# Seven-product blocks in four gated FFNs and two mixers: two of four weight sums moved from VectorE to accumulating transfers, with another order of products and another first block

## The chip, the cores and the metric

The kernel runs on one core of a Trainium2 chip. The metric is the device time of one execution in microseconds (us). Its engines are TensorE (PE in the profile, with PEld for its weight loads), VectorE (DVE), ScalarE (ACT), GpSimd (POOL) and SyncE (SP). They run their own instruction queues and wait for one another by semaphores. SP, ACT and POOL can each issue transfers (DMA), which 16 DMA engines carry out.

## What is computed

Two transformer blocks over one sequence of 256 tokens of width 1024, all in float32. Each block is half a gated FFN, a mixer and half a gated FFN, with an RMS norm ahead of each; the second one ends in a norm.

```python
x = x + 0.5 * swiglu(rms_norm(x, ffn1_norm), w_gate, w_up, w_down)     # FFN 1
x = x + concat(attention_with_top_64(h), pooled(h)) @ w_out            # mixer 1, h = rms_norm(x) @ w_in
x = x + 0.5 * swiglu(rms_norm(x, ffn2_norm), ...)                      # FFN 2
x = x + 0.5 * swiglu_2(rmsnorm(x, ffn1_norm_2), ...)                   # FFN 3
x = x + hybrid_mixer(rmsnorm(x, mix_norm_2), ...)                      # mixer 2
x = x + 0.5 * swiglu_2(rmsnorm(x, ffn2_norm_2), ...)                   # FFN 4
x = rmsnorm(x, final_norm_2)

def swiglu(x, w_gate, w_up, w_down):                                   # 1024 -> 2816 -> 1024
    return (silu(x @ w_gate) * (x @ w_up)) @ w_down
```

## The kernel before

Tokens lie in two tiles t of 128, the width in 8 tiles k of 128. Float32 precision is had from float32r matmuls: every operand is split into a rounded part `hi` (ACT copies it, L80) and the rest `lo` (DVE subtracts, L81), and a product is three matmuls (`mm3`, L83). `weights` (L65) loads 128x2048 float32, 1 MB, by SP into one of two `raw` buffers, and `parts` splits it into one of three pairs of `whi` and `wlo`.

An FFN (`ffn`, L300) has gate and up columns in blocks j of 512 (the last, j = 5, of 256 gate and 256 up columns). A plain block takes gate (G) and up (U) in halves c of four k: one weight load, 24 matmuls of 512 columns for each half, four halves in all, two for block 5. `plain` (L321) is a generator that hands back after each half. Blocks 1 and 3 are done by `quad` (L156): G and U times two halves of the width, two by two blocks, with seven products of 12 matmuls in place of eight. It loads b11, b12, b22, b21 as w11, w12, w22, w21 into four `block` buffers, forms sums of them on DVE (L180, L183, L188, L197) and multiplies them with the sums and differences of x that `combined` (L136) left split in `xc`. Results are joined by DVE (L186 to L202). It hands back after each product. `ORDER` (L35) lists for two groups of blocks whose next step comes: 0 the seven-product block, 1 and 2 the plain ones.

Ahead of the groups the first block, j = 0, is done: G half 0, U half 0, G half 1, U half 1, with `combined` before the last. In FFN 1 `cold_start` (L279) does G half 0 in four pieces as they land. `gated` (L308) takes silu, scales by `rstd` and multiplies; `turned` (L205) transposes the product (eight 128x128 transposes with `ident`) and splits it into `act`. It is put off by `later` and done by a `flush` some steps on. Then the down product runs over `act` in six weight loads for each 512 columns, and `add` (L251) adds it to X.

`mixer1` (L403) projects by `products`, loads tables (`mixer1_tables`, L384) by POOL, forms q and k tables on DVE (L397, L400), and applies the rope (L382) to the index projections. `rsqrt` (L96) ends in a POOL operation. The last lines of `run` (L810 to L828) scale by the final norm and store in four pieces by SP.

The kernel is written for a framework that gives each engine its queue, sets all semaphores and may put an instruction ahead of others of the text where its operands are there earlier; buffers of one tag are given out as they come free.

Of the kernel before, what the change touches and what calls it, by code (L numbers as in the profile page):

```python
# [17 lines left out]
P = 128  # L18
T = 256
# [22 lines left out]
class Block:  # L42
# [81 lines left out]
    def rows(self, accs, w, x, k0, nk, last, n=512):  # L124

        for t in range(2):
# [29 lines left out]
    def quad(self, pool, b, x, xc):  # L156
# [32 lines left out]
        ps = product(of_xc(2), self.parts(w12))  # L189
        tt(y21, ps, y12, op=ALU.add)  # L190
        tt(y12, y12, y22, op=ALU.add)
        tt(y22, y21, y22, op=ALU.add)
        yield
        ps = product(of_xc(3), self.parts(w22))
        tt(y12, ps, y12, op=ALU.add)
# [4 lines left out]
        yield  # L200
        ps = product(of_x(1, 0), self.parts(w21))
        tt(y11, ps, y11, op=ALU.add)  # L202
        return [y11, y21], [y12, y22]
# [47 lines left out]
    def add(self, accs, f, scale, following):  # L251
# [3 lines left out]
        for t in range(2):  # L255
# [4 lines left out]
        for t in range(2):  # L260
            self.squares(t, f)
# [16 lines left out]

    def cold_start(self, accs, src):  # L279

        nc = self.nc
        raw = self.block()
        hi = self.wsp.tile([P, 2048], F32R, tag="whi", name="whi")
        lo = self.wsp.tile([P, 2048], F32R, tag="wlo", name="wlo")
        xT = self.block().rearrange("p (k t) -> p k t", t=T)
        self.hT = self.big.tile([P, KD, 2, T], F32R, tag="hT", name="hT")
        for k in range(4):
            s = slice(k * 512, k * 512 + 512)
            if k % 2 == 0:
                nc.sync.dma_start(xT[:, k : k + 2, :], self.a["xT"][:, k : k + 2, :])  # L290
            nc.sync.dma_start(raw[:, s], src[:, s])
            self.feed(k, xT[:, k, :], "ffn1_norm")
            self.split(hi[:, s], lo[:, s], raw[:, s])
            for t in range(2):
                self.mm3(accs[t], self.both(self.hT[:, k, :, t * P : t * P + P]), (hi[:, s], lo[:, s]), k == 0, False)
        nc.sync.dma_start(xT[:, 4:8, :], self.a["xT"][:, 4:8, :])
        for k in range(4, KD):
            self.feed(k, xT[:, k, :], "ffn1_norm")

    def ffn(self, n, following, first=False):  # L300
        nc, a = self.nc, self.a
        gu, d, d_end = a[f"gu{n}"], a[f"d{n}"], a[f"de{n}"]
        with self.stage(4), self.tc.tile_pool(name="act", bufs=1) as pool:
# [4 lines left out]
            def gated(j, gs, us):  # L308
# [8 lines left out]
                self.later(lambda: self.turned(act, prs, 4 * j), 2)  # L317
# [18 lines left out]
            def seven(j):  # L336
                gated(j, *(yield from self.quad(pool, [[gu[2 * j + i, c] for i in range(2)] for c in range(2)], self.hT, xc)))


            G = two()  # L340
            if first:
                self.cold_start(G, gu[0, 0])
            else:
                self.token_major(G, gu[0], 512, 0)
            self.flush()
            U = two()
            self.token_major(U, gu[1], 512, 0)
            self.flush()
            self.token_major(G, gu[0], 512, 1)
            if first:  # L350
                nc.sync.dma_start(self.ident, a["ident"])
                for t in range(2):
                    nc.sync.dma_start(self.X[t], a["x"][t])
                    for f in range(2):
                        self.squares(t, f)
            r = self.rstd()
            self.combined(xc, self.hT)
            self.token_major(U, gu[1], 512, 1)
            gated(0, G, U)

            for order, blocks in ORDER:
                steps = [seven(j) if kind == "s" else plain(j) for kind, j in blocks]
                for i in order:
                    next(steps[i], None)
                    self.flush(2 - (blocks[i][0] == "s"))
            for f in range(2):
                accs = [self.ps() for _ in range(2)]
                for c in range(6):
                    self.rows(accs, self.weights(d[f, c] if c < 5 else d_end[f]), act, 4 * c, 4 if c < 5 else 2, KF - 1)
                    self.flush(2)  # L370
                self.add(accs, f, 0.5, following)
# [12 lines left out]
    def mixer1_tables(self):  # L384
        nc, a, c1 = self.nc, self.a, self.c1
        load = lambda name, shape: self.load(c1, name, shape, nc.gpsimd)
        cosq, sinq = load("cosq", [P, 2, 64]), load("sinq", [P, 2, 64])
        self.cosi, self.sini = load("cosi", [P, 2, 32]), load("sini", [P, 2, 32])
# [536 lines left out]
```

## Time and profile before

| | us |
|---|---|
| device time, median of 3 runs | 1125.61 (1124.76 to 1126.65) |
| the profiled execution, device time | 1126.87 |
| its span, first to last instruction | 1125.1 |
| PE busy | 1079.1 (96%), 5154 matmuls |
| DVE busy | 790.3 (70%) |
| ACT busy | 568.1 (50%) |
| POOL busy | 22.0 (2%) |
| mean granted clock of TensorE | 0.985 |
| transfers | 201.76 MB, 179 GB/s over the span |

A busy PE counts overlapping matmuls once, so that a stretch with gaps shorter than a matmul counts as busy; the number of matmuls in a stretch tells more. Granted clock 1.00 is 2.4 GHz, 0.5 is 1.2 GHz.

### The profile page before, as it was taken

The numbers are of one execution on the slowest core, as the hardware profiler recorded it, in microseconds if no ns is written. First come the engines' busy times: TensorE is split into PE (matmuls) and PEld (weight loads), VectorE is DVE, ScalarE is ACT, GpSimd is POOL, SyncE is SP. The second block draws the span as 40 slices with busy tenths as digits, with TensorE's granted clock in tenths as the row PEclk, the third lists the DMA queues.
The fourth block names the chain that finished last, engine by engine and source line by source line (L and its number), as shares of the span: only waits on it lengthen the run. The fifth ranks groups of instructions, "written<-read, shape, count | busy, mean of one in ns | idle before, by whom it ended". The sixth has DMA issues, their size and how long they took to land.

```text
span 1125.1 us, 12742 instructions
## 1 busy us (share of the span) xinstructions
PE 1079.1 (96%) x5154; PEld 895.0 (80%) x5154; DVE 790.3 (70%) x785; ACT 568.1 (50%) x632; POOL 22.0 (2%) x42
## 2 busy tenths in 40 slices
PE   6899999899999999998999999999999998999996
PEld 4788888778876788886777888999888887778785
DVE  6889744597589986458997555677645467998543
ACT  6465534568355654434565444543444345566432
POOL 0000000220000000000000000000000000000000
PEclk8999999989999999999999999999999999999999
DMA  7562655543264435545626555454555436443552
GB/s 292 209 250 75 223 180 204 217 150 113 75 262 150 184 116 188 201 173 224 227 110 230 201 187 206 162 195 168 187 180 195 150 137 237 157 181 112 202 189 76
DMA packets 30539, 201.76 MB, mean 179 GB/s; under 512 B 3680, under 2 KB 3824, under 8 KB 7568
## 3 DMA queue, kind: packets, MB, share of 16 engines
q1 hardware_dynamic: 29520, 198.04, 48.3%
q0 software_dynamic: 960, 2.90, 0.7%
q8 instruction: 40, 0.66, 0.2%
q14 instruction: 19, 0.16, 0.0%
HBM read 199.88 MB, written 1.05 MB: 179 GB/s over the span
## 4 chain that ended last, share of the span: by engine, by line
PE 61%; issue 20%; DVE 11%; ACT 4%; DMA 3%; POOL 1%; SPq 0%; ACTq 0%; POOLq 0%; DVEq 0%
PE acc L87 11%; PE acc L88 11%; PE acc L86 11%; PE tmp L87 8%; PE tmp L86 8%; PE tmp L88 8%; DVE wlo L81 5%; ACT whi L80 3%; DMA raw<-in_gu 1%; PE tmp L211 1%; DMA qg<-in_q_norm 1%; PE tmp L94 1%; PE acc L94 1%; DVE pr L315 1%; DMA block<-in_xT 1%
## 5 line engine op out<-in xcount | busy, mean ns | idle before, releaser
L81 DVE TENSOR_TENSOR wlo<-raw,whi 128x2048 fp32r<-128x2048 f32 (+1 forms) x130 | 288.9, 2223 | 175.0 <-ACT whi L80 174.9
L80 ACT ACTIVATE whi<-raw 128x2048 fp32r<-128x2048 f32 (+1 forms) x130 | 242.3, 1864 | 262.2 <-PE tmp L88 114.1
L86 PE MATMUL acc<-whi,hT 128*128 128x512 f32 x536 | 214.7, 404 | 10.4 <-ACT whi L80 9.8
L81 DVE TENSOR_TENSOR wlo<-block,whi 128x2048 fp32r<-128x2048 f32 (+2 forms) x87 | 189.8, 2194 | 48.3 <-ACT whi L80 47.1
L87 PE MATMUL acc<-wlo,hT 128*128 128x512 f32 x536 | 214.0, 399 | 3.0 <-DVE wlo L81 3.0
L88 PE MATMUL acc<-whi,hT 128*128 128x512 f32 x536 | 213.0, 399 | 0.3 <-DVE hT L224 0.3
L80 ACT ACTIVATE whi<-block 128x2048 fp32r<-128x2048 f32 (+2 forms) x87 | 159.3, 1842 | 104.2 <-PE tmp L88 30.5
L86 PEld LDWEIGHTS acc<-whi,hT 128*128 128x128 f32 x536 | 103.0, 193 | 33.6 <-ACT whi L80 11.0
L87 PEld LDWEIGHTS acc<-wlo,hT 128*128 128x128 f32 x536 | 103.2, 193 | 25.7 <-DVE wlo L81 4.5
L88 PEld LDWEIGHTS acc<-whi,hT 128*128 128x128 f32 x536 | 103.0, 192 | 22.3 <-DVE hT L224 1.1
L87 PE MATMUL tmp<-wlo,hT 128*128 128x512 f32 (+1 forms) x216 | 83.4, 386 | 1.9 <-DVE wlo L81 1.9
L86 PE MATMUL tmp<-whi,hT 128*128 128x512 f32 (+1 forms) x216 | 83.7, 389 | 0.4 <-ACT whi L80 0.3
L88 PE MATMUL tmp<-whi,hT 128*128 128x512 f32 (+1 forms) x216 | 82.6, 385 | 0.0
L86 PE MATMUL tmp<-whi,act 128*128 128x512 f32 x198 | 77.3, 391 | 0.0
L88 PE MATMUL tmp<-whi,act 128*128 128x512 f32 x198 | 77.1, 389 | 0.0
L87 PE MATMUL tmp<-wlo,act 128*128 128x512 f32 x198 | 77.0, 389 | 0.0
L86 PE MATMUL acc<-whi,act 128*128 128x512 f32 x154 | 60.4, 392 | 0.0
L87 PE MATMUL acc<-wlo,act 128*128 128x512 f32 x154 | 60.1, 390 | 0.0
L88 PE MATMUL acc<-whi,act 128*128 128x512 f32 x154 | 60.0, 389 | 0.0
L86 PE MATMUL tmp<-whi,xc 128*128 128x512 f32 x128 | 51.4, 401 | 8.2 <-ACT whi L80 5.5
L87 PE MATMUL tmp<-wlo,xc 128*128 128x512 f32 x128 | 51.4, 401 | 1.6 <-DVE wlo L81 1.5
L88 PE MATMUL tmp<-whi,xc 128*128 128x512 f32 x128 | 50.8, 397 | 0.0
(257 smaller groups left out, 1584.9 us busy)
## 6 DMA issues: line engine op xcount, KB each, us to landing
raw<-in_gu SPq DMA_DIRECT2D x55, 1024.0 KB, 4.8
raw<-in_d SPq DMA_DIRECT2D x40, 1024.0 KB, 4.8
block<-in_gu SPq DMA_DIRECT2D x32, 1024.0 KB, 6.0
raw<-in_de SPq DMA_DIRECT2D x8, 512.0 KB, 3.4
block<-in_w_out SPq DMA_DIRECT2D x4, 1024.0 KB, 5.0
raw<-in_w_out SPq DMA_DIRECT2D x4, 1024.0 KB, 4.9
block<-in_w_cx SPq DMA_DIRECT2D x4, 1024.0 KB, 5.0
raw<-in_w_cx SPq DMA_DIRECT2D x4, 1024.0 KB, 4.9
```

Source lines behind the costliest of these rows:

```text
L80: self.nc.scalar.activation(hi, x, AF.Copy)
L81: self.nc.vector.tensor_tensor(lo, x, hi.bitcast(F32), op=ALU.subtract)
L86: mm(ps, lhsT=a[0], rhs=b[0], start=start, stop=False)
L87: mm(ps, lhsT=a[0], rhs=b[1], start=False, stop=False)
L88: mm(ps, lhsT=a[1], rhs=b[0], start=False, stop=stop)
L94: self.nc.tensor.matmul(ps, lhsT=a, rhs=b, start=start, stop=stop)
L211: self.nc.tensor.transpose(pt[:, i, :], x[t][:, i * P : i * P + P], self.ident)
L315: nc.vector.scalar_tensor_tensor(pr, us[t], r[:, t : t + 1], sg, op0=ALU.mult, op1=ALU.mult)
```

## The change

In `quad`, w12 + b22 and w11 + b12 are formed by two transfers that POOL issues with an add into the buffer, in place of DVE sums; the other two sums stay on DVE. The products come in the order 1, 7, 3, 2, 5, 6, 4 of their old tags (p1, p7, p3, p2, p5, p6, p4), and ACT copies four of them out of PSUM in place of two. Block 5 moves from the end of the second group to the front of the first, `combined` behind its first half, and `gated` of a quad puts off its transposes by 4 in place of 2. In FFN 1 G and U of the first block are both done in pieces, interleaved for the first half of the width; fourteen matmuls of a tile of ones stand ahead of everything. `gains` and the first piece are issued by ACT. Six tables of mixer 1 go by SP, the indexer's first. The output product of mixer 1 and the last two weight loads of FFN 4 are done by token tile, and the final norm by token tile, with one store by ACT.

```diff
+WARM = 14
 ORDER = (
-    ((0, 0, 1, 0, 0, 0, 1, 0, 0, 1, 1), (("s", 1), ("p", 2))),
-    ((0, 0, 1, 0, 0, 0, 1, 0, 0, 1, 1, 2, 2), (("s", 3), ("p", 4), ("p", 5))),
+    ((2, 2, 0, 1, 0, 0, 1, 0, 0, 1, 0, 0, 1), (("s", 1), ("p", 2), ("p", 5))),
+    ((0, 1, 0, 0, 1, 0, 0, 1, 0, 0, 1), (("s", 3), ("p", 4))),
 )
...
-        w11, w12, w22, w21 = self.block(b[0][0]), self.block(b[0][1]), self.block(b[1][1]), self.block(b[1][0])
+        more = lambda w, src: nc.gpsimd.dma_start(w, src, accum_op=ALU.add)
+        (b11, b12), (b21, b22) = b
+        w11, w12, w22, w21 = self.block(b11), self.block(b12), self.block(b22), self.block(b21)
+        more(w12, b22)
         y11 = copy(product(of_x(0, 0), self.parts(w11)), "p1")
+        more(w11, b12)
         yield
-        tt(w11, w11, w12, op=ALU.add)
-        y22 = copy(product(of_xc(0), self.parts(w11)), "p5")
+        p7 = copy(product(of_xc(2), self.parts(w12)), "p7")
+        yield
+        y12 = copy(product(of_xc(3), self.parts(w22)), "p3")
+        yield
+        y21 = p("p2")
+        tt(y21, product(of_x(1, 0), self.parts(w21)), y11, op=ALU.add)
+        y11, v = y21, y11
+        yield
+        p5 = copy(product(of_xc(0), self.parts(w11)), "p5")
         yield
         tt(w11, w11, w22, op=ALU.add)
-        ps = product(of_xc(1), self.parts(w11))
-        y12, y21 = p("p6"), p("p7")
-        tt(y12, ps, y11, op=ALU.subtract)
-        yield
-        tt(w12, w12, w22, op=ALU.add)
...
+        tt(v, product(of_xc(1), self.parts(w11)), v, op=ALU.subtract)
+        tt(p7, p7, v, op=ALU.add)
+        tt(v, v, p5, op=ALU.add)
+        tt(p5, p7, p5, op=ALU.add)
+        tt(y12, y12, v, op=ALU.add)
         yield
         tt(w11, w11, w21, op=ALU.add)
-        ps = product(of_x(1, 1), self.parts(w11))
-        tt(y21, ps, y21, op=ALU.subtract)
...
+        tt(p7, product(of_x(1, 1), self.parts(w11)), p7, op=ALU.subtract)
+        return [y11, p7], [y12, p5]
...
+    def warm_up(self):
+        ps = self.bank("tmp")
+        for _ in range(WARM):
+            self.mm(ps[:, :P], self.ones, self.ones)
+
     def cold_start(self, accs, src):
...
+        for c in range(2):
+            w = []
+            for i in range(2):
+                raw = self.block()
...
+            for i, k in [(i, k) for k in range(4) for i in range(2)] if c == 0 else [(i, k) for i in range(2) for k in range(4)]:
+                kd, s = 4 * c + k, slice(k * 512, k * 512 + 512)
+                raw, hi, lo = w[i]
+                if i == 0 and k % 2 == 0:
+                    xT = self.work.tile([P, 2, T], F32, tag="pr", name="xT", bufs=4)
+                    nc.sync.dma_start(xT, a["xT"][:, kd : kd + 2, :])
+                (nc.scalar if kd + i == 0 else nc.sync).dma_start(raw[:, s], src[i, c][:, s])
...
+                if i == 0:
+                    self.feed(kd, xT[:, k % 2, :], "ffn1_norm")
+                self.split(hi[:, s], lo[:, s], raw[:, s])
+                for t in range(2):
+                    self.mm3(accs[i][t], self.both(self.hT[:, kd, :, t * P : t * P + P]), (hi[:, s], lo[:, s]), kd == 0, kd == KD - 1)
+                if c == 1 and i == 0 and k == 3:
+                    nc.sync.dma_start(self.ident, a["ident"])
+                    for t in range(2):
+                        nc.sync.dma_start(self.X[t], a["x"][t])
+        for t in range(2):
+            for f in range(2):
+                self.squares(t, f)
...
-                self.later(lambda: self.turned(act, prs, 4 * j), 2)
+                self.later(lambda: self.turned(act, prs, 4 * j), wait)
...
-            self.combined(xc, self.hT)
-            self.token_major(U, gu[1], 512, 1)
+            if not first:
+                self.token_major(U, gu[1], 512, 1)
             gated(0, G, U)
             for order, blocks in ORDER:
...
+                    if n == 0 and order is ORDER[0][0]:
+                        self.combined(xc, self.hT)
...
+                if split:
+                    ws = [down(f, c) for c in (4, 5)]
+                    for t in range(2):
+                        for c in (4, 5):
+                            self.rows(accs, ws[c - 4], act, 4 * c, 4 if c < 5 else 2, KF - 1, tiles=[t])
+                        self.add(accs, f, 0.5, following, [t])
...
-        load = lambda name, shape: self.load(c1, name, shape, nc.gpsimd)
+        load = lambda name, shape, engine=None: self.load(c1, name, shape, engine)
+        self.cosi, self.sini = load("cosi", [P, 2, 32]), load("sini", [P, 2, 32])
         cosq, sinq = load("cosq", [P, 2, 64]), load("sinq", [P, 2, 64])
...
-            nc.gpsimd.dma_start(g, a[f"{n}_norm"].to_broadcast([P, HD]))
+            nc.sync.dma_start(g, a[f"{n}_norm"].to_broadcast([P, HD]))
...
-            self.rows(accs, w, mT[half], 0, 4, 3)
-            self.flush()
+            for t in range(2):
+                self.rows(accs, w, mT[half], 0, 4, 3, tiles=[t])
+                self.flush()
...
-        self.gains = self.load(self.const, "gains", [P, len(NORMS) * KD])
+        self.gains = self.load(self.const, "gains", [P, len(NORMS) * KD], nc.scalar)
+        self.warm_up()
```

## Rows read from the trace of the kernel before

**Rows 1.** The page's first part: busy us, share of the span, instructions.
```profile
PE 1079.1 (96%) x5154; PEld 895.0 (80%) x5154; DVE 790.3 (70%) x785; ACT 568.1 (50%) x632; POOL 22.0 (2%) x42
```

**Rows 2.** Stretches: length, busy (count) of PE, PEld, DVE, ACT, POOL, clock, DMA, GB/s.
```profile
0.00:38.50 38.50, 28.05 (x97) 21.81 (x97) 25.29 (x26) 21.76 (x30) 1.18 (x7) 0.91 0.84 326
38.50:53.00 14.50, 10.86 (x44) 8.48 (x43) 14.23 (x9) 8.99 (x8) 0.00 (x0) 0.88 0.20 65
...
211.00:238.00 27.00, 21.76 (x94) 16.56 (x93) 18.61 (x48) 14.78 (x53) 3.84 (x3) 0.81 0.53 204
...
335.00:420.00 85.00, 81.45 (x361) 65.15 (x360) 80.31 (x56) 50.00 (x38) 0.00 (x0) 1.00 0.41 150
337.00:353.00 16.00, 13.53 (x57) 9.58 (x56) 13.96 (x9) 10.83 (x9) 0.00 (x0) 1.00 0.20 67
...
522.00:535.00 13.00, 9.04 (x36) 6.64 (x35) 12.84 (x9) 5.17 (x5) 0.00 (x0) 0.87 0.26 101
535.00:572.00 37.00, 36.70 (x163) 29.29 (x162) 34.65 (x26) 23.03 (x17) 0.00 (x0) 1.00 0.59 227
...
616.00:625.00 9.00, 6.91 (x28) 5.24 (x27) 7.52 (x8) 5.08 (x5) 0.00 (x0) 0.81 0.66 231
...
1058.00:1116.00 58.00, 58.00 (x257) 48.02 (x256) 24.15 (x16) 16.96 (x14) 0.00 (x0) 1.00 0.39 137
```

**Rows 3.** Chain of waits, then timeline at the end: start, us, engine and line.
```profile
124.35 0.87 PE tmp L211 x8
...
1119.90 1.81 SPq L828 DMA_DIRECT2D out<-y  x4
```

**Rows 4.** Groups by line and shape: count, busy us, mean ns, idle before and releaser.
```profile
L81 DVE TENSOR_TENSOR wlo<-block,whi 128x2048 fp32r<-128x2048 f32 x81 | 184.0, 2286 | 41.9 <-ACT whi L80 40.7
L188 DVE TENSOR_TENSOR block<-block 128x2048 f32<-128x2048 f32 x8 | 18.3, 2284 | 0.1
...
L186 DVE TENSOR_TENSOR p<-tmp,p 128x512 f32<-128x512 f32 x8 | 5.5, 687 | 0.0
...
L80 ACT ACTIVATE whi<-raw 128x2048 fp32r<-128x2048 f32 x122 | 233.8, 1916 | 235.4 <-PE acc L88 99.8 <-PE tmp L88 98.0 <-DMA raw<-in_d 15.8
```

**Rows 5.** Timeline of the first 20 us: start, us, instruction, idle before and releaser.
```profile
5.55 1.30 ACT L80 ACTIVATE whi<-block 128x512 fp32r<-128x512 f32 x2 [0.39 <-DMA block<-in_gu]
...
6.23 0.80 PE L86 MATMUL acc<-whi,hT 128*128 128x512 f32 x1 [6.23 <-ACT whi L80]
...
7.55 0.63 PE L88 MATMUL acc<-whi,hT 128*128 128x512 f32 x1
...
16.64 0.73 PE L86 MATMUL acc<-whi,hT 128*128 128x512 f32 x2 [1.85 <-ACT whi L80]
19.75 0.80 PE L87 MATMUL acc<-wlo,hT 128*128 128x512 f32 x1 [2.37 <-DVE wlo L81]
```

**Rows 6.** Transfers by line: queue, count, KB each, median us from issue to landing.
```profile
block<-in_gu SPq DMA_DIRECT2D x32, 1024.0 KB, 6.0
...
band<-in_band POOLq DMA_DIRECT2D x1, 768.0 KB, 12.3
sgu_w<-in_sgu_w POOLq DMA_DIRECT2D x1, 512.0 KB, 6.0
...
qg<-in_q_norm POOLq DMA_DIRECT2D x1, 32.0 KB, 11.2
```

**Rows 7.** First mixer: timeline of POOL and DVE, and PE's longest wait.
```profile
209.94 0.53 POOL L394 DMA_DIRECT2D qg<-in_q_norm  x1
...
221.24 0.29 DVE L397 TENSOR_TENSOR qC<-cosq,qg 128x128 f32<-128x128 f32 x1 [7.58 <-DMA qg<-in_q_norm]
...
PE acc L438 <- DVE R L382: 3.8, 1, 3.8
```

**Rows 8.** Timeline of DVE in FFN 2.
```profile
359.16 2.28 DVE L197 TENSOR_TENSOR block<-block 128x2048 f32<-128x2048 f32 x1
361.36 0.68 DVE L191 TENSOR_TENSOR p<-p,p 128x512 f32<-128x512 f32 x1
```

More of the change, by code (lines that the diff above doesn't have):

```diff
@@ L121, in later, with rows @@
         self.late.append((n, f))
-    def rows(self, accs, w, x, k0, nk, last, n=512):
-        for t in range(2):
+    def rows(self, accs, w, x, k0, nk, last, n=512, tiles=(0, 1)):
+        for t in tiles:
             for k in range(k0, k0 + nk):
@@ L249, in row, with add @@
         return R
-    def add(self, accs, f, scale, following):
+    def add(self, accs, f, scale, following, tiles=(0, 1)):
         nc = self.nc
         s = slice(f * 512, f * 512 + 512)
-        for t in range(2):
+        for t in tiles:
             x = self.X[t][:, s]
@@ L259, in add @@
             return
-        for t in range(2):
+        for t in tiles:
             self.squares(t, f)
@@ L287, in cold_start @@
[L287 to L295, printed above, removed]
@@ L306, in ffn, with gated @@
             r = None
-            def gated(j, gs, us):
+            def gated(j, gs, us, wait=2):
                 prs = []
@@ L336, in seven @@
             def seven(j):
-                gated(j, *(yield from self.quad(pool, [[gu[2 * j + i, c] for i in range(2)] for c in range(2)], self.hT, xc)))
-            G = two()
+                gated(j, *(yield from self.quad(pool, [[gu[2 * j + i, c] for i in range(2)] for c in range(2)], self.hT, xc)), 4)
+            G, U = two(), two()
             if first:
-                self.cold_start(G, gu[0, 0])
+                self.cold_start((G, U), gu)
             else:
                 self.token_major(G, gu[0], 512, 0)
-            self.flush()
[L346 to L355, printed above, removed]
+                self.flush()
+                self.token_major(U, gu[1], 512, 0)
+                self.flush()
+                self.token_major(G, gu[0], 512, 1)
             r = self.rstd()
-            self.combined(xc, self.hT)
-            self.token_major(U, gu[1], 512, 1)
+            if not first:
+                self.token_major(U, gu[1], 512, 1)
             gated(0, G, U)
@@ L362, in ffn @@
                 steps = [seven(j) if kind == "s" else plain(j) for kind, j in blocks]
-                for i in order:
+                for n, i in enumerate(order):
                     next(steps[i], None)
+                    if n == 0 and order is ORDER[0][0]:
+                        self.combined(xc, self.hT)
                     self.flush(2 - (blocks[i][0] == "s"))
+            down = lambda f, c: self.weights(d[f, c] if c < 5 else d_end[f])
             for f in range(2):
-                accs = [self.ps() for _ in range(2)]
-                for c in range(6):
-                    self.rows(accs, self.weights(d[f, c] if c < 5 else d_end[f]), act, 4 * c, 4 if c < 5 else 2, KF - 1)
+                accs = two()
+                split = f == 1 and following == "final_norm_2"
+                for c in range(4 if split else 6):
+                    self.rows(accs, down(f, c), act, 4 * c, 4 if c < 5 else 2, KF - 1)
                     self.flush(2)
-                self.add(accs, f, 0.5, following)
+                if split:
[4 more added lines that the diff above has]
+                        self.add(accs, f, 0.5, following, [t])
+                else:
+                    self.add(accs, f, 0.5, following)
     def rope(self, dst, src, C, S, heads, half):
@@ L818, in run @@
                 nc.vector.tensor_tensor(y[:, s], self.X[t][:, s], fg[:, s], op=ALU.mult)
-            ys.append(y)
-        r = self.rstd()
-        for t in range(2):
             for f in range(2):
@@ L824, in run @@
                 if f:
-                    nc.vector.tensor_scalar(ys[t][:, s], ys[t][:, s], r[:, t : t + 1], None, op0=ALU.mult)
+                    nc.vector.tensor_scalar(y[:, s], y[:, s], r, None, op0=ALU.mult)
                 else:
-                    nc.scalar.activation(ys[t][:, s], ys[t][:, s], AF.Copy, scale=r[:, t : t + 1])
-                nc.sync.dma_start(self.out[t * P : t * P + P, s], ys[t][:, s])
+                    nc.scalar.activation(y[:, s], y[:, s], AF.Copy, scale=r)
+                (nc.scalar if f == 0 and t == 1 else nc.sync).dma_start(self.out[t * P : t * P + P, s], y[:, s])
 def _constants():
```

44 lines of the change are left out of this document (16 added, 28 removed).

## Prediction

> **What bounds the kernel now.** I read the page's busy table first: TensorE (PE) is busy in 1079.1 of 1125.1 us [rows 1], so the gain can only come from the 46 us in which it stands idle and from the stretches in which it runs slowly. The second view is the table of stretches. Its last long row gives the yardstick: 257 matmuls of 512 columns in 58.00 us, 0.226 us each [rows 2]. A transpose of 128 columns takes 0.109 us: eight of them start within 0.87 us [rows 3]. With these two prices the count in a stretch says what it would last without loss, and the rest is the loss. The reader is to see that the losses stand in few places: the first 38.5 us, the beginning of the seven-product blocks in each of the four FFNs, 211 to 238 us (first mixer), and the last 9 us. Everything else runs at the yardstick. The third view is VectorE (DVE) in the quad phases: 80.31 of 85.00 us busy from 335 to 420 us [rows 2]. There it sets the pace: each weight block costs it one `wlo` subtraction of 2.29 us, each weight sum another 2.28 us [rows 4], against 12 x 0.226 = 2.7 us of PE for one of the seven products. A quad asks of DVE 7 x 2.29 + 4 x 2.28 + 7 x 0.68 = 29.9 us and gives PE 19.0 us of work. Only the plain blocks beside it (4 x 2.29 = 9.2 us of DVE for 48 + 48 matmuls, 21.7 us) pay for it.
>
> **The first block.** Removed: G and U one after another, the whole-block loads of U, and the wait in between. The 96 matmuls of the first block are worth 96 x 0.226 = 21.7 us and take until 38.5, a loss of 16.8 us [rows 2]. The rows show why: the first matmul starts at 6.23 and the first dozen last 0.63 us, not 0.39 as later, which is the lower clock; PE then waits 1.85 us for a `whi` and 2.37 us for a `wlo` and is slow again [rows 5]. The change splits both halves of the block in 256 KB pieces. A pair of pieces with its `hT` costs ACT 2 x 0.65 us (half of the x2 row in [rows 5] each) and under 0.6 for the smaller `hT`, 1.9 us at most, DVE the like, against 12 x 0.226 = 2.7 us of PE, so PE paces. The transfers: 5.2 MB of pieces and `xT` and 1.1 MB of X and `ident` at the 326 GB/s of this stretch [rows 2] need 19 us after the first landing at about 4, so they are in by 24, and PE comes to its last piece at about 28. That is the cover, 3 to 4 us. With it gone each us late is a us lost. The fourteen idle products run from about 1 us: at twice 0.109 us they fill 3 us and cost nothing, because PE has no data then. What they bring the trace before doesn't show. The twelve slow matmuls at the start cost 12 x 0.226 = 2.7 us over the full pace (half the clock doubles them); the bounds are none and all of it given back, and I take half. `gains` and the first piece leave SP's queue, 0.45 us an issue [rows 3]: the start comes at some 5.7. End of the block: 5.7 + 21.7 + 1.3 + 0.8 for waits left over = 29.5. **Gain 9.0 us** (6.5 to 10).
>
> **The quad phases.** Two of four sums go to transfers: DVE loses 2 x 2.28 x 8 = 36.5 us. ACT gains two small copies a quad and is busy 50.00 of 85 us [rows 2], nothing. POOL issues 16 accumulates; one issue takes 0.53 us there [rows 7], nothing either: its other work in an FFN is the `rstd`, which comes earlier. Block 5 moves to the front of the order: its two halves, 10.9 us of PE, lie over the `combined` sums (2.29 + 4 x 0.69 + 2.29 = 7.3 us of DVE) and the loads, which before stood between the first block and the first quad. The wait of the quads' `turned` grows from 2 to 4; that of plain blocks does not, so I leave PE's waits there. Losses now, by the counts of [rows 2], eight transposes in each: FFN 1, 38.5 to 53: 14.5 - (36 x 0.226 + 0.87) = 5.5. FFN 2, 337 to 353: 16 - (49 x 0.226 + 0.87) = 4.1. FFN 3: 5.8 (522 to 535), 1.1 (535 to 572), 3.6 (616 to 625, where the DVE backlog delayed a load). FFN 4 repeats the first two: 5.7 and 1.1 (948 to 962 and 962 to 999, one row of each pair shown). With DVE's demand down to about 71 of 85 us I take back **4.5 + 4.0 + 8.5 + 5.5 = 22.5 us**, and charge 8 x 0.2 = 1.6 us for the two adjacent last products of a quad, whose sums and splits follow each other.
>
> **The accumulating transfers** are the unknown, since the trace has none. Tolerance, with PE at pace: w11 is free once product 1 is split and is needed, split, at the fifth: 4 products and 2 halves of a plain block between are 4 x 2.7 + 2 x 5.4 = 21.6, less split 4.2 and issue 0.5: 16.9 us. w12 of the second quad gets the buffer of the first one's w22, free 4.2 us ahead of product 6; up to its own product 3 x 2.7 + 2 x 5.4 = 18.9 pass, less load 6.0 [rows 6] and issue 0.5: 12.4 us. Bounds for one MB: 6.0 us (`block<-in_gu`) and 16.4 us (`band`, 768 KB in 12.3, beside full traffic) [rows 6]. Nearest is `sgu_w`, a plain load on the same queue beside weight loads: 512 KB in 6.0 us, so 12 us, just inside. I take no cost; at 16.4 us it is 4 x 4.0 = 16 us. It can't gain below nothing beyond what the sums brought. The Trainium skill says, in "DMA: Bandwidth & Descriptors", section "Rules for kernel authors", that an accumulate reads its destination and writes it later; and in the section "Bandwidth" 6.15 us for a plain MB from GpSimd, so reading twice would be an estimate of 12.3 us. No row here shows it; by it the sum stays as it is.
>
> **The tables.** In program order DVE's table products stand ahead of the rope, and wait for `qg`, issued by POOL as the tenth at 209.94 and landed 11.2 us later: DVE stands still for 7.58 us and PE then waits 3.8 us for `R` [rows 6, 7], with the clock down to a mean of 0.81 in 211 to 238 [rows 2]: 5.2 us idle and up to 5.1 us by the clock, some 8 us together. On SP the six small tables wait for the same release, the end of FFN 1, and go out within 6 x 0.45 = 2.7 us, not as the ninth to twelfth of POOL. Behind them in SP's queue stand the loads of `w_k` and `w_v`, 2.7 us later; DVE, which splits them, stands still until 221, so they are covered, and otherwise cost 2.7 us. **Gain 6.5 us** (0 to 8). Rival A is that they land as late as before. The Trainium skill speaks for it, in "DMA: Bandwidth & Descriptors", section "Issuing engines are not separate DMA queues": all queues use the same engines, and moving a transfer saves the issuing time alone.
>
> **The end.** Token half 0 gets its last 18 matmuls (4.1 us) earlier, so that after the last matmul one half's add, square, scale and store remain. Now four stores go out one after another in 1.81 us [rows 3]; two of them (0.9 us) and one scale of y fall away behind the last matmul. **Gain 1.2 us** (0.5 to 2). `project` in two halves changes an order, nothing I can price.
>
> **Sum.** 9.0 + 22.5 - 1.6 + 6.5 + 1.2 = 37.6 us. The profiled execution took 1126.87 us (span 1125.1 and 1.8 around it): 1089.3. The runs' median lies 1.26 us below it: **1088 us.**
>
> **Rivals.** A, the tables land as late as before, held up by other transfers: for it, `causal`, `band` (12.3 us [rows 6]) and `pool_w` still go out beside them; against it, nine issues of 0.53 us ahead of `qg` are 5 us of its lateness by themselves. 1088 + 6.5 = 1094.5. B, accumulates take 12.4 to 18.5 us: 1104 at 16.4. C, DVE's relief does not reach PE, because split chains (1.92 + 2.29 us) and three split buffers set the pace, not DVE's load: only start, tables and end remain, 16.7 us: 1109. For it: inside the loss of FFN 2, 337 to 353, DVE is busy in 13.96 of 16 us only; against it, 94% over 335 to 420 [rows 2]. D, **slower**: in the text the sum for product 7 stands behind five DVE operations that wait for product 6. If DVE's queue keeps that order, product 7, which follows at once, waits 0.69 + 2.28 + 1.92 + 2.29 = 7.2 us in every quad: 8 x 7.2 = 57 us, 1145; it decides from 37.6 / 8 = 4.7 us a quad on. Against it: the queue before is not in the order of the text: the sum L197 stands ahead of L191 [rows 8]. E, accumulates over 18.5 us: an FFN then loses (L - 12.4) + 2 (L - 16.9), which is 37.6 / 4 at 18.5; at 24 us, 1191.
>
> **How the numbers follow.** Forecast 0.60, A 0.12, B 0.10, C 0.09, D 0.05, E 0.04. Its own best end: 10 + 17 + 8 + 2, four post-block waits of 0.9, and FFN 2 to 4 whole, some 52 us: 1073, and a little below for what I can't price; the range reaches up to C and the tables with slow accumulates together: 1070 to 1113. D and E are left out. A measurement of this kernel tells about 0.2% (2.3 us) from no change. Faster 0.89 (all but D, E and the edge of B), within 0.02, slower 0.09.
>
> **What would show it.** The first block's 96 matmuls end near 29.5 with full pace from 8 on. From 320 to 420 DVE falls under 85% and PE has no idle over 1 us; no wait of `whi` on an accumulate. `qg` lands before 212 and DVE's 7.58 us are gone. An accumulate lands within 12 us. Wrong if PE waits on ACT or DVE ahead of product 2 (B, E) or 7 (D), or if PE idles as before with DVE idle too (C).

## The result and the profile after the change

| | before | after |
|---|---|---|
| median of the runs | 1125.19 us (4) | 1164.34 us (4; 1163.92 to 1165.23) |
| ratio | | 1.035, 95% interval 1.033 to 1.037 |
| profiled execution | 1126.87 us | 1164.37 us, span 1162.6 |

The changed kernel is 3.5% slower, where 3.3% faster was forecast. First the page: busy times, the software queue of the DMA engines (POOL's transfers), and the transfers (count, KB, median us from issue to landing). They answer [rows 1, 6].

```profile
PE 1091.6 (94%) x5182; PEld 906.6 (78%) x5182; DVE 760.8 (65%) x780; ACT 577.4 (50%) x657; POOL 33.9 (3%) x53
q0 software_dynamic: 3072, 19.42, 8.1%
...
block<-in_gu SPq DMA_DIRECT2D x32, 1024.0 KB, 6.7
block<-in_gu POOLq DMA_DIRECT2D x16, 1024.0 KB, 11.5
```

DVE did lose work (790.3 to 760.8 us), and a transfer that accumulates (POOLq) lands in 11.5 us, the 12 us of the forecast. The span is 37.5 us longer. PE is busy for 12.5 us of it: 5.65 us are the fourteen idle products, and the mean granted clock fell from 0.985 to 0.969. The other 25 us are idle time. The stretches (columns as in [rows 2]) say where:

```profile
0.00:38.50 38.50, 34.88 (x155) 28.56 (x156) 28.52 (x39) 26.08 (x42) 2.51 (x8) 1.00 0.96 350
335.00:420.00 85.00, 72.43 (x307) 58.21 (x306) 53.66 (x40) 42.95 (x38) 2.58 (x3) 0.90 0.61 195
```

The first block is better: 155 matmuls instead of 97 in 38.5 us (28 of them are the fourteen idle ones, of which the trace has two records each), and from 8 us on at the full pace. The quad phase of FFN 2 is far worse: 307 instructions of PE instead of 361 in the same 85 us, DVE busy in 53.66 us only. Two of PE's waits are new (engine, line, releaser: us, times, longest):

```profile
PE acc L87 <- ACT sg L333: 26.7, 8, 5.8
...
PE acc L87 <- ACT whi L81: 19.9, 4, 8.0
```

Eight waits on a silu: two a quad phase. Four on a split: one a phase. The timeline of PE in FFN 2 has one of each; behind each a stretch at 0.63 us a matmul, 0.43 from start to start, where the granted clock is 0.50 (350 to 357 and 399.4 to 404.5).

```profile
341.90 0.38 PE L212 MATMUL tmp<-ident,pr 128*128 128x128 f32 x2
350.30 1.22 PE L87 MATMUL acc<-whi,hT 128*128 128x512 f32 x2 [8.02 <-ACT whi L81]
...
395.63 0.39 PE L89 MATMUL acc<-whi,hT 128*128 128x512 f32 x1
399.46 0.80 PE L87 MATMUL acc<-whi,hT 128*128 128x512 f32 x1 [3.45 <-ACT sg L333]
400.06 0.63 PE L88 MATMUL acc<-wlo,hT 128*128 128x512 f32 x1
```

With each matmul of 512 columns at 0.226 us from start to start [rows 2], what lies over that adds up to: at the beginnings of the four quad phases 4.8, 12.4, 10.8 and 9.2 us (37 together), at the ends of their two groups 10.9, 8.9, 15.4 and 11.9 (47). Before, the same places lost some 37 us, beginnings and ends together.

**The wait at the beginning.** The split at 350 waits for a load. SP's queue (start, length, issues):

```profile
317.92 15.00 SPq L154 DMA_DIRECT2D block<-in_gu  x4
332.96 19.97 SPq L71 DMA_DIRECT2D raw<-in_gu  x3
```

and the transfers from 328 to 348 (queue, packets, MB, share of the 16 engines; then the landings):

```profile
q0 software_dynamic: 274, 2.10, 51.4%
q1 hardware_dynamic: 489, 3.61, 48.5%
...
raw<-in_gu SPq DMA_DIRECT2D x2, 1024.0 KB, 16.3
```

The last of a quad's four block loads waits until 332.6 for a buffer of `combined`; behind it stand the loads of block 5's second half and of block 2, issued at 332.96. They then need 16.3 us to land, beside two accumulates (POOL issues them at 328.15 and 335.72) that take 51.4% of the engines' time for 2.10 MB.

**The wait at the end.** ACT from 396 to 402:

```profile
396.06 1.91 ACT L81 ACTIVATE whi<-block 128x2048 fp32r<-128x2048 f32 x1 [3.52 <-PE acc L89]
398.07 0.72 ACT L333 ACTIVATE sg<-p,rstd 128x512 f32<-128x512 f32 x1
398.73 0.69 ACT L333 ACTIVATE sg<-acc,rstd 128x512 f32<-128x512 f32 x1
401.59 0.69 ACT L333 ACTIVATE sg<-acc,rstd 128x512 f32<-128x512 f32 x1 [2.17 <-DVE pr L335]
```

The next plain block needs the four `acc` banks (PSUM buffers) of block 2. The silu of block 2 (`sg<-acc`) could read G long before, but stands behind the quad's (`sg<-p`), which waits for the last join of the quad on DVE (L203, 397.35 to 398.03). At 399.42 the first bank is read, and at 399.46 PE goes on. At the end of the second group the down projection waits for banks in the same way. The last join (L203), the first (L196) and the sum for product 7 (L202) on DVE:

```profile
381.07 2.29 DVE L202 TENSOR_TENSOR block<-block 128x2048 f32<-128x2048 f32 x1
...
389.81 0.68 DVE L196 TENSOR_TENSOR p<-tmp,p 128x512 f32<-128x512 f32 x1
...
397.35 0.68 DVE L203 TENSOR_TENSOR p<-tmp,p 128x512 f32<-128x512 f32 x1
```

### The profile page after: what moved, and what is told of

Its sections match the earlier page's. It is cut to its first block, busy times and chain, and to the rows that moved or that the text cites. A ratio compares the mean times of both kernels' runs of the same rounds, so it can differ in the third digit from the quotient of the medians.

```text
span 1162.6 us, 12919 instructions
## 1 busy us (share of the span) xinstructions
PE 1091.6 (94%) x5182; PEld 906.6 (78%) x5182; DVE 760.8 (65%) x780; ACT 577.4 (50%) x657; POOL 33.9 (3%) x53
## 4 chain that ended last, share of the span: by engine, by line
PE 70%; DVE 12%; DMA 7%; ACT 6%; issue 4%; SPq 0%; POOL 0%; POOLq 0%; ACTq 0%; DVEq 0%
PE acc L87 15%; PE acc L88 15%; PE acc L89 15%; DVE wlo L82 7%; PE tmp L87 6%; PE tmp L89 6%; PE tmp L88 6%; ACT whi L81 5%; DMA raw<-in_gu 4%; PE tmp L212 2%; DVE block L202 2%; DMA raw<-in_d 2%; ACT sg L333 1%; DMA block<-in_gu 1%; PE acc L95 1%
## 5 line engine op out<-in xcount | busy, mean ns | idle before, releaser
L87 PE MATMUL acc<-whi,hT 128*128 128x512 f32 (+1 forms) x568 | 226.9, 401 | 33.9 <-ACT whi L81 19.9
L82 DVE TENSOR_TENSOR wlo<-block,whi 128x2048 fp32r<-128x2048 f32 (+2 forms) x99 | 198.4, 2013 | 78.8 <-ACT whi L81 78.6
L88 PE MATMUL acc<-wlo,hT 128*128 128x512 f32 (+1 forms) x568 | 223.7, 394 | 5.1 <-DVE wlo L82 5.1
L89 PE MATMUL acc<-whi,hT 128*128 128x512 f32 (+1 forms) x568 | 222.9, 393 | 2.8 <-DVE hT L225 2.8
L87 PEld LDWEIGHTS acc<-whi,hT 128*128 128x128 f32 x568 | 109.1, 193 | 58.5 <-ACT whi L81 21.4
L87 PE MATMUL acc<-whi,act 128*128 128x512 f32 x352 | 140.7, 400 | 12.9 <-ACT sg L333 12.9
L88 PE MATMUL acc<-wlo,act 128*128 128x512 f32 x352 | 139.5, 396 | 0.0
L89 PE MATMUL acc<-whi,act 128*128 128x512 f32 x352 | 139.2, 395 | 0.0
L89 PEld LDWEIGHTS acc<-whi,hT 128*128 128x128 f32 x568 | 108.5, 191 | 25.0 <-DVE hT L225 3.3
L87 PEld LDWEIGHTS acc<-whi,act 128*128 128x128 f32 x352 | 67.4, 192 | 28.2 <-ACT sg L333 14.5
L89 PEld LDWEIGHTS acc<-whi,act 128*128 128x128 f32 x352 | 67.4, 191 | 14.3
L88 PEld LDWEIGHTS acc<-wlo,act 128*128 128x128 f32 x352 | 67.4, 192 | 13.5
L87 PE MATMUL tmp<-whi,hT 128*128 128x512 f32 x184 | 76.4, 415 | 1.6 <-ACT rel L480 1.6
L88 PE MATMUL tmp<-wlo,hT 128*128 128x512 f32 x184 | 75.2, 409 | 0.3 <-DVE wlo L82 0.3
L89 PE MATMUL tmp<-whi,hT 128*128 128x512 f32 x184 | 73.7, 400 | 0.0
## 6 DMA issues: line engine op xcount, KB each, us to landing
block<-in_gu POOLq DMA_DIRECT2D x16, 1024.0 KB, 11.5
```

The lines of the kernel that those rows point to most:

```text
L82: self.nc.vector.tensor_tensor(lo, x, hi.bitcast(F32), op=ALU.subtract)
L87: mm(ps, lhsT=a[0], rhs=b[0], start=start, stop=False)
L88: mm(ps, lhsT=a[0], rhs=b[1], start=False, stop=False)
L89: mm(ps, lhsT=a[1], rhs=b[0], start=False, stop=stop)
```

## Experiments

All times are medians beside 1125 to 1126 us of the kernel before on the same chip. The order within each engine is laid out by a planner from its own estimates, so an edit can shift neighbours too; where it did not, that is said.

**1. The transfers.** Without them, and with plain loads in their place (two of the four sums are then left out, so the quads compute something else):

```diff
-        more = lambda w, src: nc.gpsimd.dma_start(w, src, accum_op=ALU.add)
+        more = lambda w, src: nc.gpsimd.dma_start(w, src)
```

> The changed kernel with the two accumulating transfers of each quad left out and nothing in their place (two of the four weight sums are missing, so the quads compute something else). Theory T (transport): the accumulates take the DMA engines from the weight loads, and the loads for block 5 and its successor stand late in SP's queue; then the losses at the beginning of the quad phases (342.0 and after in FFN 2, 12.4 us; 544.8, 10.8 us; 987.7, 9.2 us; some 33 us together) go and the time is near 1131 us, with the losses at the quads' ends still there. Theory G (gate): the losses stand where the next block's PSUM banks wait for a silu that stands behind the quad's own silu in ACT's queue; then nothing of that goes and, the losses at the beginnings being DVE's, the time stays at 1155 to 1164 us.

> The changed kernel with plain loads of the same block into the same tile where the accumulating transfers stand (the sums are missing, so the quads compute something else). If it is the adding itself that costs (8 KB packets of 679 ns against 353 ns), the time comes within 5 us of the run without any transfer there; if it is only that 16 MB more are moved, or the place in the queues, it stays within 5 us of 1164 us.

Measured: 1136.96 and 1137.07 us. The second run has the same instructions in the same order on every engine; only the adding is gone, and with it 27.3 us. The transfers in the same 20 us of FFN 2 (327.5 to 347.5):

```profile
q0 software_dynamic: 288, 2.10, 25.8%
...
raw<-in_gu SPq DMA_DIRECT2D x3, 1024.0 KB, 7.6
```

The same 2.10 MB take half the engine time (25.8 for 51.4%), and the loads land in 7.6 us, not 16.3. PE's waits on the silu stay:

```profile
PE acc L87 <- ACT sg L333: 27.2, 8, 6.2
```

**2. The silu.** The quad's `gated` goes one step later, behind the neighbour's:

```diff
-                gated(j, *(yield from self.quad(...)), 4)
+                y = yield from self.quad(...)
+                yield
+                gated(j, *y, 4)
```

(and one more 0 at the end of each order).

> The changed kernel, where only the silu and the product of a quad's own block are issued one step later, behind those of the plain block beside it; PE's order stays. Theory G: the losses at the ends of the two groups (87.1, 135.5, 395.6, 445, 596.8, 646.3, 1038.1, 1088.7; 47 us with the slow clock behind them) fall to under 10 us and the time to 1120 to 1130 us. Theory T: these losses are the transport's as well, and the time stays at 1158 us or above.

Measured: 1120.92 us (ratio 0.996, 0.995 to 0.998). SP's and POOL's queues have the same order as before the edit; PE's, DVE's and ACT's shift in places. 43.4 us come back, and the losses at the ends fall from 47 to under 4 us. ACT's timeline in FFN 2 has G read as soon as it is complete:

```profile
363.67 0.69 ACT L333 ACTIVATE sg<-acc,rstd 128x512 f32<-128x512 f32 x1 [0.32 <-PE acc L89]
368.21 0.67 ACT L333 ACTIVATE sg<-acc,rstd 128x512 f32<-128x512 f32 x1
...
386.50 0.72 ACT L333 ACTIVATE sg<-p,rstd 128x512 f32<-128x512 f32 x1 [1.58 <-DVE pr L335]
```

The losses at the beginnings stay (some 38 us), as the waits on the silu stayed in experiment 1. So there are two costs, and each stays when the other goes. If they add, 1164.3 - 27.3 - 43.4 = 1093.6; the two edits were not run together, but experiment 6 comes to 1093.7 by another way.

**3. The quad alone, in the old order of steps**, with the transfers and with plain loads:

> The kernel before with the new quad alone (two accumulating transfers, new product order, sums split between DVE and transfers); its first block, its order of steps (two plain halves behind the last product of a quad), tables and end as before. The run that left the accumulates out was 27.4 us faster than the changed kernel, and the run that issued the quad's silu behind the neighbour's 43.4 us. If both costs lie in the new quad wherever it stands: 1150 us or above. If the second lies in the new order of steps, with only one plain half behind the last product: some 1125 + 27 = 1152 us less what DVE's relief brings (up to 22 us by the prediction), 1130 to 1150 us. If the accumulates hurt only at the place that the new order gives them: 1105 to 1120 us.

> The kernel before with the new quad alone, as in the run of 1153.8 us, but with plain loads of the same blocks where the accumulating transfers stand (two sums are missing, so the quads compute something else). If all that the new quad costs in the old order of steps is the adding in the transfers: 27 to 35 us less, 1119 to 1127 us. If the new order of its products costs too, with DVE's sums and splits of the last two products behind each other, 1135 us or above.

Measured: 1153.80 and 1141.31 us. There the adding costs 12.5 us, and the quad 16 us without it. No wait on `sg` is left among PE's longest, so the silu's place is a matter of the new order of steps. In the run with plain loads PE's longest waits at the beginnings are 5.5 us, in FFN 3 and FFN 4, where it was 2.5 before; the beginning of FFN 2 loses some 4 us less. Inside the four phases PE loses some 3 to 4 us more in each, mostly in gaps of under 1 us. Which part of the new quad makes them was not taken apart. Two plain halves behind the last product, as before, do away with one cost but not with all.

**4. The rest alone**: old quad, old order, old place of `combined`; first block, tables, projection and end as changed.

> The changed kernel with the quad, the order of the steps, the place of the combined activations and the wait of 2 taken back to the kernel before; first block, tables by SP, output projection by halves and the end as changed. By the prediction's terms 9.0 + 6.5 + 1.2 = 16.7 us under the kernel before: near 1108.5 us. If the tables bring nothing (rival A), 1115 us. If the first block's gain is given back at the quad that follows, 1117 us or more.

Measured: 1122.82 us, ratio 0.997 (0.996 to 0.999): 2.7 us of 16.7. By the starts of the down projections, FFN 1 came 5.3 us sooner to its down projection, FFN 3 and the first mixer were within 2 us, and from FFN 3's last down matmul to FFN 4's first it took 4.1 us more. That is the second mixer:

```profile
931.35 1.03 PE L212 MATMUL tmp<-ident,m 128*128 128x128 f32 x8
934.00 0.51 PE L87 MATMUL tmp<-whi,mT 128*128 128x512 f32 x1 [1.61 <-ACT mT L81]
...
936.44 0.51 PE L89 MATMUL tmp<-whi,mT 128*128 128x512 f32 x1 [1.22 <-DVE mT L82]
```

(PE, changed kernel.) Before, the same product ran on `acc` and lost under 0.5 us. The down projections take banks with `two()`, no longer through `ps()`, which counts them; so every later stage got the other half of the banks.

> The changed kernel with the quad's silu behind the neighbour's, and with the down projections counting PSUM banks through the common counter again, as the kernel before did: the changed kernel takes their banks outside the counter, so that every later stage gets the other half of the banks. In the second mixer the last output product then stands on the four banks that the transposes use, and PE loses 3.4 us at 901 to 905 that it did not lose before. If the banks are the cause, that loss goes and the time falls from 1120.9 us by 3.4 us, or a little more: 1114 to 1118 us. If it comes from the loads or the splits, 1120 to 1122 us.

Measured: 1122.99 us, no gain in the whole. The base is the run with the silu moved (1120.92 us), which this edit starts from. The loss at the second mixer went (3.40 to 0.37 us), but the first mixer took 4.7 us longer (108.7 for 104.0 us from FFN 1's last down matmul to the last matmul of the output product). The mechanism holds and the sum does not: the counter helps one stage and hurts the other.

**5. DVE's sums for the transfers**, all with the silu moved: both, one, and one in the first quad of a phase only (the lines shown are the last one's).

```diff
-        more(w12, b22)
+        if not crowd:
+            more(w12, b22)
         y11 = copy(product(of_x(0, 0), self.parts(w11)), "p1")
         more(w11, b12)
+        if crowd:
+            tt(w12, w12, w22, op=ALU.add)
```

> The changed kernel with the quad's silu issued behind the neighbour's, and with both sums back on DVE in place of the accumulating transfers (product order as changed). With it the run that only moved the silu (1120.9 us) still loses 7.6 + 4.4 us at 335 in FFN 2, 9.7 in FFN 3, 8.2 in FFN 4 and some 6 after the first block. Theory T, the accumulates cause these: they go, less up to 10 us for 36 us more work on DVE: 1094 to 1105 us. If DVE needs the relief that the change gave it, 1110 us or above.

> The changed kernel with the quad's silu behind the neighbour's, and with one of the two accumulating transfers back on DVE: the sum for product 7, which is issued at the beginning of each quad among the loads; the other, needed three products later, stays a transfer. If the accumulates cost by their engine time wherever they stand, half of the 27 us comes back: near 1107 us. If it is the crowd at the beginning of a quad phase, nearly all: 1094 to 1100 us, at or under the run with both sums on DVE. If one accumulate beside the loads is enough to delay them, 1115 us or above.

> As the run with one sum on DVE (1109.9 us; the quad's silu behind the neighbour's), but the sum for product 7 is on DVE only in the first quad of a phase, where the loads crowd; in the second quad both sums are accumulating transfers as in the changed kernel. That run still lost 2.9 + 0.8 us at the end of the first quad of each FFN (87.6, 381.2, 568.1, 991.2), where DVE is behind; with both sums transferred there was 0.4 us. If an accumulate hurts only in the crowd at the beginning of a quad phase, and DVE's relief counts in the second quad: 4 x 3.3 = 13 us less, near 1096 us. If accumulates cost wherever they stand, 1108 us or above.

Measured: 1122.83, 1109.86 and 1094.96 us. With both sums on DVE the beginnings in FFN 2 to 4 lose only 2 to 4 us, but around the end of the first quad PE loses 6 to 9 us to DVE: the relief was needed, as forecast, and the first theory (1094 to 1105) fell. Transfers in the second quad cost nothing that the trace shows, and the last split has the best of both.

**6. By which way.** If the loads are late because of their place in SP's queue, it should help to issue the block loads elsewhere, here by POOL. The base is again the run with the silu moved (1120.92 us):

```diff
-        w11, w12, w22, w21 = self.block(b11), self.block(b12), self.block(b22), self.block(b21)
+        def take(src):
+            w = self.block()
+            nc.gpsimd.dma_start(w, src)
+            return w
+
+        w11, w12, w22, w21 = take(b11), take(b12), take(b22), take(b21)
```

> As the run with the quad's silu behind the neighbour's and both sums by transfers (1120.9 us), but the four block loads of each quad are issued by POOL ahead of the accumulates, not by SP, so that no load of the plain blocks stands in SP's queue behind a block load that waits for its buffer. If the place in SP's queue makes the loads of block 5 late, the losses at the beginnings of the quad phases (12.0 us in FFN 2, 9.7 in FFN 3, 8.2 in FFN 4, some 5 in FFN 1) go: 1092 to 1100 us. If it is the transfer engines' time that the accumulates take beside those loads, 1115 us or above; slower than 1121 us if the accumulates, now behind four loads, come too late.

Measured: 1093.73 us, 27.2 under the base, with all sixteen accumulates. FFN 2's phase, which begins some 7 us sooner than in the changed kernel (columns as in [rows 2]):

```profile
327.00:412.00 85.00, 84.97 (x386) 69.26 (x384) 68.63 (x48) 52.76 (x46) 5.14 (x8) 1.00 0.65 198
```

PE is busy in 84.97 of 85 us. The load of block 5's second half goes out at 316.75, block 2's at 322.76, ahead of both accumulates (326.41 and 328.76); they land at 321.5 and 328.3. With the blocks on SP they went out at 325.83 and 326.35 and landed at 340.6 and 343.1. But the first accumulate began 5 us later too. A first attempt to delay it alone did not: the transfer went out ahead of the operation that was to hold it (1127.91 us), and says nothing of the question; why it took 7 us more than the base was not looked into. Held by a read of its destination:

> The run before this one did not do what it was meant to: its wait stood behind the first accumulating transfer on POOL, which went out at 321.55 as ever, so that it measured nothing of the question. Here the small operation on POOL reads the transfer's own destination as well, so that the accumulate has to come after it, once the combined activations are complete. Base: 1120.9 us (quad's silu behind the neighbour's, both sums by transfers, block loads on SP). If the blocks on POOL were quick (1093.7 us) only because the first accumulate then began some 5 us later: 1093 to 1100 us. If because the plain blocks' loads left SP's queue: 1112 us or above, PE still waiting 5 us or more for a whi at the beginning of each quad phase. In between if both count.

Measured: 1120.59 us. POOL's timeline shows that it was held, and PE's waits that this was not it:

```profile
324.53 0.19 POOL L182 TENSOR_TENSOR seen<-block,xc 128x1 f32<-128x1 f32 x1 [19.53 <-DVE xc L82]
325.03 0.93 POOL L178 DMA_DIRECT2D block<-in_gu  x1 [0.30 <-POOL seen L182]
```

```profile
PE acc L87 <- ACT whi L81: 13.2, 5, 4.4
```

The longest wait shrinks (7.4 to 4.4 us, under the 5 us expected if the queue alone counts) and the time does not: the down projections of FFN 1 and FFN 2 take 1.5 and 1.4 us longer instead. So the later accumulate explains none of the 27.2 us. What is left, and what the landings above show, is the place in SP's queue: it turns the accumulates' engine time into a loss of PE.

**7. The small parts**, on the run with the sums by group (1094.96 us, the base here): table products on POOL (those of S in the same way as the one shown), with that the bank counter moved on ahead of the second mixer only, and no idle products.

```diff
-            nc.vector.tensor_tensor(C, cosq, ...)
+            nc.gpsimd.tensor_tensor(C, cosq, ...)
...
+            self.banks += 4
             self.mixer2("ffn2_norm_2")
```

> As the run with the sums by group, and the six products of the rope tables on POOL in place of DVE. In the changed kernel they stand in DVE's queue ahead of the split of the w_k block and of four hT halves, and wait until 212.6 for the row of gains that SP has issued at 205.7; PE stands for 3.1 us on those halves. If that is what is left of the tables' cost, DVE goes on at once and 3 to 5 us fall away against the run with the sums by group. If PE waits for the rope or for the loads next, 0 to 1 us.

> As the run with the table products on POOL, and the counter of PSUM banks moved on by four ahead of the second mixer, so that this stage has the banks that it had in the kernel before. By the run that counted the banks as before, the loss of 3.4 us at the second mixer's last output product goes: 3 us under the run with the table products on POOL. If the bank was not the cause there, no difference.

> As the run with the sums by group, without the fourteen idle products. By the prediction they give back half of 2.7 us: 1.4 us slower than that run, with the first dozen matmuls of the first block at 0.45 us each and the low clock up to about 12 us, as in the kernel before. If the idle products bring nothing, the same; if the whole 2.7 us (or more, because later stretches of the first block fall to the low clock as well), up to 5 us slower.

Measured: 1092.51, 1088.21 and 1098.04 us (ratios 0.970, 0.967 and 0.975, each within 0.003; the first and the third overlap with the base's 0.971 to 0.976). The traces are clearer. PE's wait on an `hT` half in the first mixer, 3.2 us in the base, is not among its waits with the products on POOL, and the first mixer takes 98.9 instead of 104.0 us (same two matmuls as in point 4); the 3.4 us in the second mixer are 0.36 with the counter moved. Without idle products the first block begins at 0.43 us from start to start, which is the pace at a granted clock of 0.50 further above (the trace's clock records begin only at 12.65 us, so the clock column reads 1.00 here). PE's timeline:

```profile
6.77 0.80 PE L87 MATMUL acc<-whi,hT 128*128 128x512 f32 x1 [6.77 <-ACT whi L81]
7.49 0.80 PE L88 MATMUL acc<-wlo,hT 128*128 128x512 f32 x1
8.09 0.63 PE L89 MATMUL acc<-whi,hT 128*128 128x512 f32 x1
...
12.73 0.39 PE L88 MATMUL acc<-wlo,hT 128*128 128x512 f32 x1
```

**8. Together**: block loads, table products on POOL, the counter, the silu moved.

> As the run with the four block loads of each quad issued by POOL (1093.7 us; quad's silu behind the neighbour's, both sums by transfers), with the table products on POOL and the bank counter moved on by four ahead of the second mixer. Those two brought 2.5 and 4.3 us where the sums were split by group; if they add here, 1086 to 1088 us. If the three edits, all on POOL's queue, delay each other (table products behind block loads of the next FFN), 1092 us or above.

Measured: 1087.50 us, ratio 0.966 (0.964 to 0.968), as fast as the best of point 7 within their spread. PE is busy in 1065.5 us, 98% of the span. Its longest wait left is again one on a silu (line, releaser: us, times, longest):

```profile
PE acc L87 <- ACT sg L338: 6.9, 1, 6.9
```

It stands at 29 us in FFN 1, and is 4.9 us long in the run with the blocks on POOL alone. The first block's silu could start when `rstd` is there, at 25.9, but ACT does it at 35.55, behind four splits, two of which wait for loads. In the run with only the silu of the quads moved it is done at 25.68, ahead of them. Putting it ahead here was not tried.

## Why the prediction was wrong

**The step that failed is first the paragraph on the quad phases.** Its sentence "ACT gains two small copies a quad ..., nothing" priced ACT by its load (50 of 85 us) and not by its order: the quad's silu stands in that queue ahead of the neighbour's, and in the new order of steps only one plain half, 5.4 us, is left behind the last product, where there were two in the first group and four in the second. The joins of a quad, all moved to its end (L196 to L203), take DVE from 389.81 to 398.03 between the splits: 8.2 us, longer than that half. Price: 43.4 us, for which the sum had nothing (its 1.6 us stood for the sums and splits of the last two products). I had asked who waits for the last product (rival D), but not who waits for the banks that a silu behind it frees. D itself did not happen: DVE's queue had the sum for product 7 at 381.07, ahead of the joins.

**"I take no cost" for the transfers** failed otherwise than its rivals B and E: the landing was right (11.5 us for 12; 8.3 to 13.1), the tolerances held, and PE waits for no accumulate. The price was borne by others: twice the engine time, beside loads that stand late in SP's queue. 27.3 us, in a place that the sum had not looked at: block 5 and `combined` were moved past each other, and the fourth block load waits for a buffer of `combined`, with block 5's load behind it. The Trainium skill says in "DMA: Bandwidth & Descriptors", section "Rules for kernel authors", that an accumulate reads its destination and writes it later; the doubled engine time agrees with that. The Trainium skill says on the same page, section "Issuing engines are not separate DMA queues", that another issuing engine saves the issuing time alone. The 27.2 us of the blocks on POOL came from the order in a queue, which that sentence does not price; of the transfers' own speed no run here says anything against it.

The result looks like the sign given for rival C, PE idle with DVE idle too, but PE waits on loads and on the silu's place, not on a split chain: with the loads in time and the silu moved the same quads keep it busy (84.97 of 85 us).

**DVE's relief was right, and undervalued**, as far as it can be told from the rest of the quad phase. From FFN 2's last down matmul to FFN 3's first it took 132.9 us before and 142.5 after the change; with both costs out of the way (block loads on POOL) 120.1. The forecast's 8.5 less 0.4 gives 124.8. Block 5's new place is in these 12.8 us too. Both sums on DVE were 13 us slower than one (1122.83 against 1109.86).

**The first block** came out, in part by luck: the last of its 96 matmuls starts at 28.92 (end at 29.5 forecast), but the first starts at 6.75, not 5.7 (6.23 before), and only 0.7 us are lost on the way, not 2.1. And 3.3 us are lost right behind, from 28.9 to 33.7: the split of `combined`, two products behind the silu and the split of block 5 stand behind each other on DVE (27.80 to 33.6). With the old quads 5.3 us of 9.0 reach the down projection. The idle products brought about 3 us (3.0 us of slow matmuls in the trace without them), where I took half of 2.7. They fill 5.65 us and not the 3 us worked out, since each has two records 0.21 us apart; it cost nothing, because the first operands are there at 6.7 with them and without.

**The tables** brought 1 to 2.5 us of 6.5: from FFN 1's last down matmul to the last of the mixer's output product it took 106.4 us before, 105.5 with the old quads and 103.9 in the changed kernel, with the mixer's other changes in both. DVE's wait for `qg` fell from 7.58 [rows 7] to 3.9 us (DVE's timeline of the changed kernel, then PE's wait):

```profile
212.59 0.29 DVE L422 TENSOR_TENSOR qC<-cosq,qg 128x128 f32<-128x128 f32 x1 [3.92 <-DMA qg<-in_q_norm]
```

```profile
PE acc L89 <- DVE hT L225: 2.8, 1, 2.8
```

I assumed that an earlier landing takes the whole wait away. But SP issues `qg` at 205.68, only 4.3 us sooner, it lands 6.8 us later, and now four `hT` halves stand behind the products in DVE's queue. **The end** brought 0.4 of 1.2 us (last down matmul to the end of the span: 8.86 to 8.47), and nothing in the run with the old quads (8.92).

**Not seen at all**: `accs = two()` in the down projections, 3 us in the second mixer by way of a counter.

With both costs and the small parts mended, the kernel takes 1087.5 us. That the forecast was 1088 is partly chance: its terms for the tables and the end were too large and that for DVE too small. The lower end of its range does not come out of its own terms either (the 17 us in it is named nowhere else), which has no part in the miss.

## What to carry to other kernels

Price a reordered step by who stands behind it in each engine's queue, not by that engine's load: a silu that waits for a late result held PSUM banks of a block that had been complete for long, on an engine that was half idle. A transfer that adds in place took twice the engine time of a plain one here, at the expense of the other loads; put no load that may wait for a buffer ahead of loads that PE needs next. And a helper that counts buffers is part of every stage that runs later: an edit that goes around it moves them all.

## What the runs showed of the hardware

An accumulating transfer of 1 MB from POOL lands in 11.5 us (plain in its place: 6.3) and takes twice the engine time (51.4 for 25.8% of 20 us). While two of them and the weight loads run, the core moves 286 GB/s at full engine share, 322 with plain loads and a share of 0.84. POOL needs 0.86 us to issue one, 0.53 for a plain load of the same shape (medians).
